# Written order around the norms, and the MLP up projection's products of high and low token parts 512 columns wide, with one pool of seven PSUM banks

## Chip, cores and metric

The program runs on one core of a Trainium2 chip. The metric is the device time of one launch in microseconds (us). Three runs of the kernel before gave 2601.47, 2604.80 and 2607.71 us; the median, 2604.8 us, is the time to compare with.

## What is computed

The reference is one inference step of a two-layer backbone in fp32 on 256 tokens: 128 context tokens (group g = 0) and 128 sample tokens (g = 1), width 2048. In each layer, cut to what matters here:

```
h   = x * (1 + scale1[g]) + shift1[g]          # from adaLN, six vectors per layer and group
mix = concat(attention(h @ w_in), hgrn2(h @ w_in))
y   = LayerNorm(alpha * x + gate1[g] * (mix @ w_o))
h2  = y * (1 + scale2[g]) + shift2[g]
f   = relu(h2 @ w_up) ** 2                     # 2048 -> 8192
x   = LayerNorm(alpha * y + gate2[g] * (f @ w_down))
```

The six adaLN vectors are `c @ w_mod + b_mod` for the two groups' conditioning vectors. The output is the last x and the new attention cache and scan states.

## The kernel before

**Products.** Every fp32 product is made of three fp32r products: an operand is split into a high part (rounded to fp32r) and a low part (the rest), and TensorE adds high·high, high·low and low·high into one PSUM tile. Weights come in items of 1 MB, two halves of 128x1024 each: DMA into `raw`, then `split` casts the high half on ScalarE (`wh`, L1328) and subtracts it on VectorE (`wl`, L1329). An item is 512 rows by 512 columns of a weight; a `Unit` is the items kg = 0 to 3 of one block of 512 columns. All items stand in one list, `seq`, and the loop at the end of the program walks through it; `main_ahead` puts the split of the next item ahead of the products of this one, as long as `raw` tiles (10) are free.

**Two kinds of unit.** In kind "T" (`mm_tile`, L445, L447, L448) the weights are loaded into the array and the 256 tokens move: per item 16 pairs of output block m and row block k, with three products of 256 columns each. The MLP's up projection and part of the in-projection are of this kind. In kind "N" (`n_tile`, L457 to L459) the tokens are loaded and 512 weight columns move: 24 products per item. w_o and the down projection are of this kind. Accumulators come from a pool of three PSUM banks (`accp`); one bank belongs to the adaLN products (`modp`), four to everything else (`sdp`).

**Order in a layer.** 13 units of in-projection with attention and scans as side tasks, w_o (in two passes over two items each), norm 1, MLP (four times four up units and four down units), norm 2. After the last layer norm 2 is `ln_last`. A w_o or down unit ends in `add_gated` or `d_down`: gate (L896), residual sum (L901), `bn_stats` (L891). There are three norms with `ln_mod`: norm 1 of layer 0, norm 2 of layer 0, norm 1 of layer 1, called first, second and third norm below. `ln_stat` aggregates the statistics (L909, and 1/sqrt at L621 to L627). Then for each quarter n of the width and each group: `ln_mod` normalises (L942), transposes on TensorE (L947), applies scale and shift (`scale_shift`: L929 on VectorE for group 0, L931 on ScalarE for group 1) and splits (`split_act`, L408 and L409). Quarter n is the token operand for the item kg = n of the next unit. All four quarters are written ahead of that unit.

**Other work.** adaLN products are items in the same list: `Mod` on TensorE (L203, `psm`, four products of 512 columns per 1 MB item) and `ModH` on VectorE (L266, `ma`). Rates spread them over the units; `flush` puts what a norm needs ahead of it, and `GAP` puts six of them after the first item behind a norm. `ln_out` is a side task that applies the norm's own gain and bias to the eight normalised tiles (16 VectorE operations of 128x512, L1013 and L1014), from rows that GpSimd's queue loads into two `G` tiles (L1007, L1008).

**Order on the engines.** SyncE and GpSimd run in the order of the program text. The orders of TensorE, VectorE and ScalarE are set by the framework's scheduler, apart from `ln_last`, which is written out.

## Time and profile before

| | before |
|---|---|
| median of three runs | 2604.8 us |
| the profiled execution | 2595.31 us |
| its span | 2593.4 us |
| TensorE busy (PE) | 2508.7 us, 97% |
| weight loads (PEld) | 2150.2 us, 83% |
| VectorE busy (DVE) | 1849.1 us, 71% |
| ScalarE busy (ACT) | 1227.5 us, 47% |
| mean granted TensorE clock | 0.989 |

The profile is that of one execution; its time is 9.5 us under the median of the runs. PE time is that of matmuls, PEld that of the weight loads that go beside them. A matmul's listed duration holds its way through the array, so neighbours overlap; what one costs in a row of them is the distance of starts.

### The profile page before, as it was taken

Reading aid. Unit: us, or ns where it says so; the run is one execution under the profiler, and the core shown is the slowest. Engines: PE = TensorE matmul, PEld = TensorE weight load, DVE = VectorE, ACT = ScalarE, POOL = GpSimd, SP = SyncE. Lnnn points to the kernel's source line nnn. Section 1 sums busy time; section 2 is a strip of 40 time slices with the busy share of each in tenths; the row PEclk is TensorE's granted clock in tenths of the full one; section 3 lists DMA queues with packets and bytes.
Section 4 is the critical chain, followed back from the end, with each engine's and each line's share of the span. In section 5 each row is a group of like instructions: output and inputs, shape, how many; then the busy total and the mean of one; then the engine's idle time right before and its main releaser. Section 6 shows DMA issues by size and latency. Waiting matters only on the chain.

```text
span 2593.4 us, 41149 instructions
## 1 busy us (share of the span) xinstructions
PE 2508.7 (97%) x16276; PEld 2150.2 (83%) x16276; DVE 1849.1 (71%) x2332; ACT 1227.5 (47%) x1703; POOL 105.0 (4%) x188
## 2 busy tenths in 40 slices
PE   7999899999999999999999999999899999999996
PEld 4787777768989879879877989788798998998985
DVE  3455778679887777887777788868865565666656
ACT  3434565435545444444435666744544454443542
POOL 2000000000000000000000010001000000000002
PEclk9999999999999999999999999999999999999998
DMA  9889778989987787887878576566576666666663
GB/s 357 271 285 321 268 246 284 325 277 359 315 295 274 267 292 269 285 276 263 288 234 292 193 243 197 193 221 223 187 235 218 212 215 217 217 200 227 204 206 115
DMA packets 192304, 652.77 MB, mean 252 GB/s; under 512 B 22720, under 2 KB 25344, under 8 KB 192112
## 3 DMA queue, kind: packets, MB, share of 16 engines
q1 hardware_dynamic: 177680, 614.56, 69.1%
q0 software_dynamic: 11488, 32.91, 4.3%
q8 instruction: 127, 2.08, 0.3%
q10 hardware_dynamic: 2944, 2.69, 0.3%
q14 instruction: 65, 0.53, 0.1%
HBM read 643.19 MB, written 6.88 MB: 251 GB/s over the span
## 4 chain that ended last, share of the span: by engine, by line
PE 61%; issue 28%; DMA 5%; DVE 4%; ACT 1%; POOL 0%; SPq 0%; POOLq 0%; DVEq 0%; ACTq 0%
PE acc L445 9%; PE acc L447 9%; PE acc L448 9%; PE acc L457 9%; PE acc L459 9%; PE acc L458 9%; DMA raw<-in_w_mod_dram 2%; PE psm L203 2%; DVE wl L1329 1%; PE psm L223 1%; DMA out_nsf_dram<-lf 1%; PE pI L757 1%; PE pX L780 1%; DMA raw<-in_w_in_dram 0%; PE pO L818 0%
## 5 line engine op out<-in xcount | busy, mean ns | idle before, releaser
L1328 ACT CAST wh<-raw 128x1024 fp32r<-128x1024 f32 x784 | 821.7, 1049 | 1065.3 <-PE acc L459 456.2
L1329 DVE TENSOR_TENSOR wl<-raw,wh 128x1024 fp32r<-128x1024 f32 x784 | 953.6, 1222 | 416.1 <-ACT wh L1328 397.1
L445 PE MATMUL acc<-hh,wh 128*128 128x256 f32 x3072 | 878.4, 286 | 3.0 <-DVE q L608 1.7
L448 PE MATMUL acc<-hh,wl 128*128 128x256 f32 x3072 | 871.3, 284 | 5.5 <-DVE wl L1329 5.5
L447 PE MATMUL acc<-hl,wh 128*128 128x256 f32 x3072 | 871.4, 284 | 0.0
L445 PEld LDWEIGHTS acc<-hh,wh 128*128 128x128 f32 x3072 | 589.9, 192 | 40.9 <-issue 31.2
L448 PEld LDWEIGHTS acc<-hh,wl 128*128 128x128 f32 x3072 | 589.9, 192 | 6.5 <-DVE wl L1329 6.5
L447 PEld LDWEIGHTS acc<-hl,wh 128*128 128x128 f32 x3072 | 590.2, 192 | 0.9 <-issue 0.2
L266 DVE SCALAR_TENSOR_TENSOR ma<-raw,stat,ma 128x1024 f32<-128x1024 f32 x300 | 378.6, 1281 | 95.0 <-DMA raw<-in_w_mod_dram 91.2
L458 PE MATMUL acc<-wl,fh 128*128 128x512 f32 x1024 | 399.4, 390 | 4.7 <-DVE wl L1329 4.7
L457 PE MATMUL acc<-wh,fh 128*128 128x512 f32 x1024 | 400.6, 391 | 1.8 <-DVE Z L1241 1.8
L459 PE MATMUL acc<-wh,fl 128*128 128x512 f32 x1024 | 398.9, 390 | 0.0
L457 PEld LDWEIGHTS acc<-wh,fh 128*128 128x128 f32 x1024 | 192.3, 188 | 51.0 <-issue 7.7
L458 PEld LDWEIGHTS acc<-wl,fh 128*128 128x128 f32 x1024 | 192.3, 188 | 45.4 <-DVE wl L1329 6.3
L459 PEld LDWEIGHTS acc<-wh,fl 128*128 128x128 f32 x1024 | 192.3, 188 | 40.0
L458 PE MATMUL acc<-wl,hh 128*128 128x512 f32 x320 | 129.4, 404 | 4.4 <-DVE wl L1329 4.4
L457 PE MATMUL acc<-wh,hh 128*128 128x512 f32 x320 | 131.3, 412 | 2.1 <-ACT hh L408 2.1
L459 PE MATMUL acc<-wh,hl 128*128 128x512 f32 x320 | 127.8, 402 | 0.0
L457 PE MATMUL acc<-wh,mxh 128*128 128x512 f32 x256 | 103.2, 404 | 0.0
L458 PE MATMUL acc<-wl,mxh 128*128 128x512 f32 x256 | 100.1, 392 | 0.0
L459 PE MATMUL acc<-wh,mxl 128*128 128x512 f32 x256 | 100.0, 392 | 0.0
L203 PE MATMUL psm<-raw,stat 128*2 128x512 f32 x640 | 95.0, 596 | 2.4 <-DMA raw<-in_w_mod_dram 2.4
(360 smaller groups left out, 1902.6 us busy)
## 6 DMA issues: line engine op xcount, KB each, us to landing
raw<-in_w_mod_dram SPq DMA_DIRECT2D x384, 512.0 KB
raw<-in_w_up_dram SPq DMA_DIRECT2D x256, 512.0 KB
raw<-in_w_down_dram SPq DMA_DIRECT2D x256, 512.0 KB
raw<-in_w_in_dram SPq DMA_DIRECT2D x208, 512.0 KB
raw<-in_w_o_dram SPq DMA_DIRECT2D x64, 512.0 KB
G<-gr POOLq DMA_DIRECT2D x48, 256.0 KB, 4.6
G<-in_lng_dram POOLq DMA_DIRECT2D x12, 256.0 KB, 5.9
G<-in_lnb_dram POOLq DMA_DIRECT2D x12, 256.0 KB, 5.7
```

The lines of the kernel that those rows point to most:

```text
L203: pe.matmul(self.ps[32 * j:32 * j + 2, :], lhsT=stat[:, k, :], rhs=raw[j // 2][:, 512 * (j % 2):512 * (j % 2) + 512], start=k == 0, stop=k ...
L223: pe.matmul(self.ps[32 * j:32 * j + 2, :], lhsT=stat[:, 4 * k + j, :], rhs=raw[j // 2][:, 512 * (j % 2):512 * (j % 2) + 512], start=k == 0 ...
L266: dve.scalar_tensor_tensor(self.acc[g], raw[h], c, self.acc[g], ALU.mult, ALU.add)
L445: pe.matmul(ps, lhsT=w0, rhs=hi[:, k], start=f and k == 0 and m % 2 == 0, stop=False, skip_group_check=True)
L447: pe.matmul(ps, lhsT=w0, rhs=lo[:, k], start=False, stop=False, skip_group_check=True)
L448: pe.matmul(ps, lhsT=w1, rhs=hi[:, k], start=False, stop=e and k == 3 and m % 2 == 1, skip_group_check=True)
L457: pe.matmul(ps, lhsT=hi[:, k, gs], rhs=wh[k], start=f and k == 0, stop=False)
L458: pe.matmul(ps, lhsT=hi[:, k, gs], rhs=wl[k], start=False, stop=False)
L459: pe.matmul(ps, lhsT=lo[:, k, gs], rhs=wh[k], start=False, stop=e and k == 3)
L757: pe.matmul(pI[:, 128 * m:128 * m + 128], lhsT=ke[:, 128 * m:128 * m + 128], rhs=qe[:, 128 * m:128 * m + 128], start=True, stop=True)
L1328: act.copy(wh, r)
L1329: dve.tensor_tensor(wl, r, wh.bitcast(F32), ALU.subtract)
```

## The change

1. The three-bank pool for accumulators is gone: accumulators come from `sdp`, which has seven banks.
2. A quarter of the token operand lies as two tiles of [128, 2 k, high or low, 256 tokens], so that the high and low tokens of one k are 512 neighbouring columns. A split of four blocks becomes two casts and two subtractions of half the size.
3. All up units but the first of each layer are of a new kind "W" (30 of 32). `w_tile` issues per pair of m and k one product of 512 columns (high weights by high and low tokens) and one of 256 (low weights by high tokens). Such a unit holds four banks; at its end ScalarE copies the low half of each (256 columns) and VectorE adds the two halves, before Relu, Square and split.
4. The last w_o unit and the last down unit of a layer are "tail" units: for group 1 their last products are issued in two halves of 256 columns, and `add_gated` follows in halves. Statistics of group 1 are always taken in halves.
5. The `flush` ahead of a norm stands before the tail unit, and no rate applies within it. From the last item of the tail unit to the last item of the following unit VectorE and ScalarE are put in written order (`ordered`). `ln_mod` is called once per quarter: quarters 0 and 1 ahead of the first item, 2 ahead of the second, 3 ahead of the third. For quarter 0 ScalarE normalises group 0 and writes the high parts from PSUM (L1002), VectorE makes scale and shift (L1007) and the low parts (L1012).

The core of the diff:

```diff
-    accp = ctx.enter_context(tc.tile_pool(name="accp", bufs=3, space=PS))
-    sdp = ctx.enter_context(tc.tile_pool(name="sdp", bufs=4, space=PS))
+    sdp = ctx.enter_context(tc.tile_pool(name="sdp", bufs=7, space=PS))
...
+    def w_tile(un, m, ks, hl, wh, wl, f, e):
+
+        if f and ks[0] == 0:
+            un.ps[m] = bank("acc")
+        ps = un.ps[m]
+        for k in ks:
+            x = hl[k // 2][:, k % 2]
+            w0, w1 = (w[k][:, 128 * m:128 * m + 128] for w in (wh, wl))
+            pe.matmul(ps, lhsT=w0, rhs=x.rearrange("p a t -> p (a t)"), start=f and k == 0, stop=False,
+                      skip_group_check=True)
+            pe.matmul(ps[:, 0:256], lhsT=w1, rhs=x[:, 0], start=False, stop=e and k == 3, skip_group_check=True)
...
+    def add_gated(key, n, g, ps, gt, first, last, tail):
+
+        for cols in halves(g) if tail else [slice(0, 512)]:
+            t = gt[:, cols]
+            dve.tensor_tensor(t, ps[:, cols], t, ALU.mult)
...
+    def ln_mod(key, AB, dst, n):
...
+        if first:
+            act.activation(y[0], y[0], AF.Identity, scale=mr[0][1], bias=nb)
+        for g in (1,) if first else (1, 0):
+            dve.tensor_scalar(y[g], y[g], mr[g][0], mr[g][1], ALU.subtract, ALU.mult)
...
+        else:
+            for c in range(4):
+                for g in (1, 0):
+                    act.activation(hl[c // 2][:, c % 2, 0, 128 * g:128 * g + 128], pt[g][:, 128 * c:128 * c + 128], AF.Identity,
+                                   scale=A[:, 4 * n + c, g:g + 1], bias=B[:, 4 * n + c, g:g + 1])
...
     def put_unit(un, rate, src=None, prate=0):
+        opening = closing = False
+        if norm:
+            key, coef, dst = norm[0][:3]
+            opening, closing = un.tail, not un.tail
         for kg in un.groups:
+            if opening and kg == un.groups[-1]:
+                AB = []
+                put_call(drain)
+                put_call(lambda: AB.append(ln_coef(*coef)))
+                put_call(lambda: ordered(True))
+                norm[0] += (AB,)
+            if closing:
+                AB = norm[0][3]
+                if kg == 0:
+                    put_call(lambda: ln_open(key))
+                    put_call(lambda: ln_mod(key, AB[0], dst, 0))
+                if kg < 3:
+                    put_call(lambda kg=kg: ln_mod(key, AB[0], dst, kg + 1))
+                else:
+                    norm.pop()
             seq.append(("main", Main(un, kg)))
+            if closing and kg == 3:
+                put_call(lambda: ordered(False))
...
-                    act.activation(r, un.ps[b], AF.Relu)
+                    if un.kind == "T":
+                        act.activation(r, un.ps[b], AF.Relu)
+                    else:
+                        low = u("e1")
+                        for j in range(2):
+                            ps, c = un.ps[2 * b + j], slice(256 * j, 256 * j + 256)
+                            act.copy(low[:, c], ps[:, 256:512])
+                            dve.tensor_tensor(r[:, c], ps[:, 0:256], low[:, c], ALU.add)
+                        act.activation(r, r, AF.Relu)
```

What this does to the engines' queues is seen at three places. In the changed kernel's numbering L988 is the normalisation on VectorE, L965 and L967 are scale and shift, L413 and L414 the split of tokens, L1086 and L1087 the operations of `ln_out`, L1435 and L1436 the split of weights, L994 the transpose.

First place: VectorE in the third norm, from the normalisation of group 1's first quarter to the second item's weights. Before (1793 and following), word for word:

```order
L942 TENSOR_SCALAR Y_17151<-Y_17151,s_17914,s_17918 128x512
L942 TENSOR_SCALAR Y_17273<-Y_17273,s_17914,s_17918 128x512
L942 TENSOR_SCALAR Y_17269<-Y_17269,s_17914,s_17918 128x512
L929 TENSOR_SCALAR ed_17948<-pt_17943,A_17909,B_17910 128x128 x4
L409 TENSOR_TENSOR hl_17928<-ed_17936,hh_17927 128x4x128
L942 TENSOR_SCALAR Y_17462<-Y_17462,s_17914,s_17918 128x512
L409 TENSOR_TENSOR hl_17928<-ed_17948,hh_17927 128x4x128
```

And now:

```order
L988 TENSOR_SCALAR Y_16319<-Y_16319,s_17269,s_17273 128x512
L1086 TENSOR_TENSOR Y_16319<-Y_16319,G_18093 128x512
L1087 TENSOR_TENSOR Y_16319<-Y_16319,G_18094 128x512
L1086 TENSOR_TENSOR Y_16315<-Y_16315,G_18093 128x512
L1087 TENSOR_TENSOR Y_16315<-Y_16315,G_18094 128x512
L1007 TENSOR_SCALAR ed_17289<-pt_17288,A_17205,B_17206 128x128
L1007 TENSOR_SCALAR ed_17295<-pt_17294,A_17205,B_17206 128x128
```

The first four operations of `ln_out` stand between the first normalisation and the first scale and shift. Before, the first of the sixteen stood behind all scale and shift operations and all token splits of the norm. In the first and third norm all sixteen now lie between the statistics and the fourth item's weights, four per quarter; in the second norm four do.

Second place: the same queue from the second item's weights into the third quarter of the third norm, now:

```order
L1436 TENSOR_TENSOR wl_17353<-raw_17043,wh_17352 128x1024
L1436 TENSOR_TENSOR wl_17357<-raw_17045,wh_17356 128x1024
L988 TENSOR_SCALAR Y_16580<-Y_16580,s_17269,s_17273 128x512
L988 TENSOR_SCALAR Y_16576<-Y_16576,s_17269,s_17273 128x512
L1086 TENSOR_TENSOR Y_16580<-Y_16580,G_18619 128x512
L1086 TENSOR_TENSOR Y_16576<-Y_16576,G_18619 128x512
L1087 TENSOR_TENSOR Y_16580<-Y_16580,G_18620 128x512
L1087 TENSOR_TENSOR Y_16576<-Y_16576,G_18620 128x512
L414 TENSOR_TENSOR ha_17414<-ed_17419,ha_17414 128x2x128
L414 TENSOR_TENSOR hb_17415<-ed_17419,hb_17415 128x2x128
L965 TENSOR_SCALAR ed_17425<-pt_17424,A_17205,B_17206 128x128 x4
L414 TENSOR_TENSOR ha_17414<-ed_17425,ha_17414 128x2x128
```

Behind the last row stands one more L414 and then the two operations of the third item's weights. So the weights of the second item stand behind all of quarter 1, those of the third behind all of quarter 2, those of the fourth behind all of quarter 3. In the first and second norm, where six adaLN items follow the first item, the weights of the second item too stand behind all of quarter 2. In all three norms TensorE has the sixteen transposes of quarters 0 and 1 ahead of the first product of the first item; those of quarter 2 stand behind that item, and in the first and second norm also behind most of the six adaLN items.

Third place: TensorE in the second item of the second up unit of layer 1, two and three pairs of m and k. Before:

```order
L445 MATMUL acc_18835<-hh_17955,wh_18823 128x256
L447 MATMUL acc_18835<-hl_17956,wh_18823 128x256
L448 MATMUL acc_18835<-hh_17955,wl_18824 128x256
L445 MATMUL acc_18848<-hh_17955,wh_18823 128x256
L447 MATMUL acc_18848<-hl_17956,wh_18823 128x256
L448 MATMUL acc_18848<-hh_17955,wl_18824 128x256
```

And now:

```order
L484 MATMUL acc_17698<-ha_17320,wh_17681 128x512
L486 MATMUL acc_17698<-ha_17320,wl_17682 128x256
L484 MATMUL acc_17703<-ha_17320,wh_17681 128x512
L486 MATMUL acc_17703<-ha_17320,wl_17682 128x256
L484 MATMUL acc_17703<-ha_17320,wh_17681 128x512
L486 MATMUL acc_17703<-ha_17320,wl_17682 128x256
```

Two products of 256 columns have become one of 512; the third is unchanged.

## Rows read from the trace of the kernel before

**Rows 1.** Page, part 1: busy us (share of the span) and instructions of each engine.

```profile
PE 2508.7 (97%) x16276; PEld 2150.2 (83%) x16276; DVE 1849.1 (71%) x2332; ACT 1227.5 (47%) x1703; POOL 105.0 (4%) x188
```

**Rows 2.** Page, part 5: costliest groups: line, engine, operation xcount | busy, mean ns | idle before.

```profile
L1329 DVE TENSOR_TENSOR wl<-raw,wh 128x1024 fp32r<-128x1024 f32 x784 | 953.6, 1222 | 416.1 <-ACT wh L1328 397.1
L445 PE MATMUL acc<-hh,wh 128*128 128x256 f32 x3072 | 878.4, 286 | 3.0 <-DVE q L608 1.7
...
L445 PEld LDWEIGHTS acc<-hh,wh 128*128 128x128 f32 x3072 | 589.9, 192 | 40.9 <-issue 31.2
```

**Rows 3.** Timeline of PE in an up unit: start, duration, line.

```profile
799.72 0.28 PE L445 MATMUL acc<-hh,wh 128*128 128x256 f32 x1
799.84 0.28 PE L447 MATMUL acc<-hl,wh 128*128 128x256 f32 x1
```

**Rows 4.** Timeline of PE around the first norm, from w_o's last products to the fourth up item.

```profile
590.07 0.39 PE L457 MATMUL acc<-wh,mxh 128*128 128x512 f32 x1
...
590.52 0.39 PE L459 MATMUL acc<-wh,mxl 128*128 128x512 f32 x1
...
602.46 0.48 PE L445 MATMUL acc<-hh,wh 128*128 128x256 f32 x2
...
621.84 0.28 PE L445 MATMUL acc<-hh,wh 128*128 128x256 f32 x1
```

**Rows 5.** The same around the second norm, to the second unit of layer 1.

```profile
1359.94 0.39 PE L459 MATMUL acc<-wh,fl 128*128 128x512 f32 x1
...
1398.62 0.28 PE L445 MATMUL acc<-hh,wh 128*128 128x256 f32 x1
```

**Rows 6.** The same around the third norm.

```profile
1836.41 0.39 PE L459 MATMUL acc<-wh,mxl 128*128 128x512 f32 x1
...
1848.06 0.51 PE L445 MATMUL acc<-hh,wh 128*128 128x256 f32 x2 [0.36 <-ACT hh L408]
...
1849.18 0.36 PE L447 MATMUL acc<-hl,wh 128*128 128x256 f32 x1
```

**Rows 7.** Busy by stretch: us, engines' busy us (instructions), granted clock, DMA share, GB/s.

```profile
591.00:603.00 12.00, 11.08 (x76) 4.17 (x69) 10.04 (x25) 5.69 (x16) 0.54 (x1) 1.00 1.02 408
603.00:640.00 37.00, 37.00 (x310) 35.19 (x308) 35.44 (x44) 24.07 (x33) 0.54 (x1) 1.00 0.98 359
640.00:980.00 340.00, 338.00 (x2109) 296.57 (x2105) 278.60 (x256) 156.52 (x174) 7.77 (x15) 1.00 0.84 289
...
1360.00:1372.00 12.00, 10.47 (x75) 3.91 (x74) 11.12 (x28) 4.84 (x13) 3.02 (x6) 1.00 0.96 348
1836.60:1849.20 12.60, 5.32 (x32) 4.71 (x31) 11.78 (x27) 5.95 (x14) 0.62 (x2) 0.73 0.56 199
```

**Rows 8.** Timeline of DVE in the third norm.

```profile
1841.05 0.26 DVE L909 BATCH_NORM_AGGREGATE s<-bs 128x2 f32<-128x24 f32 x1
...
1842.82 2.83 DVE L942 TENSOR_SCALAR Y<-Y,s,s 128x512 f32<-128x512 f32 x6
1845.56 1.37 DVE L929 TENSOR_SCALAR ed<-pt,A,B 128x128 f32<-128x128 f32 x4
```

**Rows 9.** Groups by shape, as in rows 2.

```profile
L266 DVE SCALAR_TENSOR_TENSOR ma<-raw,stat,ma 128x1024 f32<-128x1024 f32 x300 | 378.6, 1281 | 95.0 <-DMA raw<-in_w_mod_dram 91.2 <-ACT ma L264 3.6
...
L1014 DVE TENSOR_TENSOR Y<-Y,G 128x512 f32<-128x512 f32 x16 | 10.9, 689 | 1.0 <-DMA G<-in_lnb_dram 1.0
...
L863 DVE TENSOR_TENSOR Z<-Z,Z 128x256 f32<-128x256 f32 x8 | 3.1, 422 | 0.1
```

**Rows 10.** Timeline of POOL behind the first norm.

```profile
589.94 0.54 POOL L1007 DMA_DIRECT2D G<-in_lng_dram  x1 [8.81 <-DVE Y L901]
592.66 0.54 POOL L1008 DMA_DIRECT2D G<-in_lnb_dram  x1 [2.19 <-DVE Y L901]
```

**Rows 11.** Page, part 6: loads of those rows: xcount, KB, median us to landing.

```profile
G<-in_lnb_dram POOLq DMA_DIRECT2D x12, 256.0 KB, 5.7
```

More of the change, by code (lines that the diff above doesn't have):

```diff
@@ L48, with __init__ @@
 class Unit:
-    def __init__(self, kind, src, act, done, groups=range(4)):
+    def __init__(self, kind, src, act, done, groups=range(4), tail=False):
         self.kind = kind
+        self.tail = tail
         self.src = src
@@ L427, in mm_tile @@
                     between()
-                n_tile(un, g, range(4), hi, lo, wh, wl, f, e)
+                if g == 1 and un.tail:
+                    for h in range(2):
+                        n_tile(un, g, range(4), hl, wh, wl, f, e, slice(256 * h, 256 * h + 256))
+                else:
+                    n_tile(un, g, range(4), hl, wh, wl, f, e)
             return
@@ L449, in mm_tile, with n_tile @@
+                    pe.matmul(ps, lhsT=w1, rhs=x[:, 0], start=False, stop=e and k == 3 and m % 2 == 1,
                               skip_group_check=True)
[L451 removed]
+    def n_tile(un, g, ks, hl, wh, wl, f, e, cols=slice(0, 512)):
         if f and ks[0] == 0:
[L453 to L454 removed]
+            un.ps[g] = bank("acc")
+        ps = un.ps[g][:, cols]
         gs = slice(128 * g, 128 * g + 128)
+        skip = un.tail
@@ L886, in gate_chunk, with halves, stats @@
         return t
-    def stats(key, n, g):
-        if n == 0:
-            bst[key, g] = sp.tile([128, 24], F32, tag="bs", name=nm("bs"), bufs=4)
-        dve.bn_stats(bst[key, g][:, 6 * n:6 * n + 6], yt[key, n, g])
-    def add_gated(key, n, g, ps, gt, first, last):
-        t = gt
-        dve.tensor_tensor(t, ps, gt, ALU.mult)
-        y = yt[key, n, g]
-        if first:
-            dve.scalar_tensor_tensor(y, y, ALPHA, t, ALU.mult, ALU.add)
-        else:
-            dve.tensor_tensor(y, y, t, ALU.add)
-        if last:
-            stats(key, n, g)
+    def halves(g):
+        return [slice(0, 512)] if g == 0 else [slice(0, 256), slice(256, 512)]
+    def stats(key, n, g, h=0):
+        m = len(halves(g))
+        if n == 0 and h == 0:
+            bst[key, g] = sp.tile([128, 24 * m], F32, tag=f"bs{g}", name=nm("bs"), bufs=2)
+        c0 = 6 * (m * n + h)
+        dve.bn_stats(bst[key, g][:, c0:c0 + 6], yt[key, n, g][:, halves(g)[h]])
+    def add_gated(key, n, g, ps, gt, first, last, tail):
+        for cols in halves(g) if tail else [slice(0, 512)]:
+            t = gt[:, cols]
+            dve.tensor_tensor(t, ps[:, cols], t, ALU.mult)
+            y = yt[key, n, g][:, cols]
+            if first:
+                dve.scalar_tensor_tensor(y, y, ALPHA, t, ALU.mult, ALU.add)
+            else:
+                dve.tensor_tensor(y, y, t, ALU.add)
+            if last and tail:
+                stats(key, n, g, cols.start // 256)
+        if last and not tail:
+            for h in range(len(halves(g))):
+                stats(key, n, g, h)
     def ln_stat(key):
```

149 lines of the change are left out of this document (90 added, 59 removed).

## The prediction, written before the changed kernel ran

> **What bounds the kernel now.** I read the shares of busy time first: TensorE is busy for 97% of the span, VectorE for 71%, ScalarE for 47% [rows 1]. So time is won by making TensorE's work shorter, and lost wherever TensorE is made to stand; an idle microsecond of it is hardly ever given back. Next the groups by line, for what fills TensorE: the largest group has 3072 products of 256 columns, and it stands for three such lines, with a weight load of 192 ns for each [rows 2]. Listed durations (286 ns) overlap, so I take prices from distances of starts: 0.12 us for a product of 256 columns [rows 3], and 0.225 to 0.23 for one of 512 (590.07 to 590.52 is two) [rows 4]; I use 0.227. The weight load is longer than 0.12, yet the products follow each other at 0.12, so it is hidden.
>
> Then the busy time by stretch, for where TensorE does not run. In the MLP it does (338.0 of 340 us), with VectorE at 278.6 [rows 7]. In the first and second norm it hardly stops either (11.08 and 10.47 of 12 us), because adaLN products fill the hole; VectorE is the fuller engine, with 35.44 of 37 us in the unit behind the first norm. In the third norm, where none are left, TensorE works 5.32 of 12.6 us and its granted clock is 0.73 there, while VectorE works 11.78 [rows 7]. What decides around a norm is thus VectorE's queue.
>
> Last the timeline of the three norms, for the length of each stretch from the last product ahead of the norm (its start plus 0.23: 590.75, 1360.17, 1836.64) to the end of the unit behind it. First norm: the fourth item starts at 621.84 and has 48 products, 5.8 us, so 627.6; 36.9 us [rows 4]. Second: the next unit's first product is at 1398.62; 38.5 us [rows 5]. Third: two products from 1848.06, then 190 at 0.12 from 1849.18, so 1872.0; 35.3 us [rows 6]. Together 110.7 us.
>
> **Term 1, wider products.** 30 units of 4 items with 16 pairs of m and k are 1920 pairs of 256-column products that become one of 512. Each saves 2 x 0.12 - 0.227 = 0.013 us [rows 3, 4], or 25 us in all. Both distances fit a fixed 0.013 us per product beside the columns' own time, and 1920 products go. I take -25.
>
> The Trainium skill, "TensorE: Matmul & The Clock Gate", section "Wait — 56ns, not 53.3ns?", has a rule that speaks against so much: start to start is the column count over 2.4 GHz plus 2.5 ns. By it the two prices would be 109 and 216 ns and the term only -4.8 us, an estimate from that page. The trace disagrees: its starts lie 120 ns apart.
>
> **Term 2, the evacuation of the wide units.** Per unit four VectorE additions of 256 columns, for which the nearest row is 0.422 us [rows 9]: 1.7 us, 51 us over 30 units, with as many ScalarE copies. It lies in VectorE's idle time in the MLP (61 of 340 us idle, rows 7; a unit is 22 us, 15 of them in a stretch of some 700). The cover holds as long as a bank is free in time: a unit takes four of seven banks, so the next unit's fourth bank waits for the first of this one. That bank is complete a quarter of an item's walk, about 2 us, before the unit ends, and wanted 2 us after, so about 4 us stand for one copy and one addition. Bounds: 0, and 15 us if each of the 30 units waits half a microsecond; I take +2, near the lower one. The first-unit kind, the split of tokens in smaller pieces and the merged pool elsewhere I cost at nothing: they are hidden beside the same products, with 5 us either way for the in-projection's side tasks, which now draw banks from the same pool.
>
> **Term 3, tail units.** Three units (and the final one) issue 12 more products each at 0.013: +0.6. In return the last gate, sum and statistics run in halves; but both halves lie in one bank and the order has them all behind the unit's last product, so nothing runs beside TensorE. At the end of the kernel nothing else moves.
>
> **Term 4, the written stretch.** The fourth item of the unit behind a norm needs `wl`, and in VectorE's queue everything of the norm now stands ahead of that, the operations of `ln_out` too. In order, an operation of the queue can't pass another, so the sum of the queue is a floor. Prices in a run: a mean less 0.05 of overlap, or a timeline's group over its count. For the third norm: 6 halves x 0.37 [rows 9] = 2.2; from the aggregate to the first normalisation 1.77 [rows 8], with the second aggregate and the bias 2.0; 7 normalisations at 2.83 / 6 = 0.47, 3.3; 20 scale and shift operations at 1.37 / 4 = 0.34, 6.8 [rows 8]; 16 subtractions of 256 columns at 0.37, 5.9; 16 `ln_out` operations at 0.64, 10.2; 6 `wl` at 1.17 [rows 2], 7.0; 2 `ma` at 1.23 [rows 9], 2.5. Sum 39.9. The fourth item can start one `wl` earlier and takes 5.8: its end is at 44.5 us or later, where it was 35.3. First norm: no `ma` but the rest, 42.0 against 36.9. Second: four `ln_out` operations and eight `ma`, 39.6, with an item of 24 x 0.227 the end is 43.9 against 38.5. (The first stretch has one adaLN item fewer than before, the second one more, which cancels.) Floor of the three: 130.4 against 110.7, **+20**.
>
> The floor has no waits in it, and the written order has several. (a) The first four `ln_out` operations stand ahead of the first scale and shift. Their rows are loaded into the tiles of the last gate: the second load was issued when the last sum was done, 1.9 us behind the last product [rows 10], and lands 5.7 later at the median [rows 11]; with three operations behind it that is about 9.5 us. Scale and shift, subtractions, two normalisations and the transposes of quarter 1 (all ahead of the first product) bring the first item to some 15 us, where it was 11.7 in the first and 11.4 to 12.5 in the third norm [rows 4, 6]. (b) From there each quarter goes round: VectorE normalises, TensorE transposes, ScalarE scales and casts, VectorE subtracts, ScalarE casts the next item's weights behind that, VectorE subtracts them. VectorE's own part is 8.7 us per quarter (2 x 0.47, 4 x 0.64, 4 x 0.34, 4 x 0.37, 2 x 1.17), with one or two microseconds of waiting up to 10.5; TensorE's part is 5.8 for the item and one for transposes, so it stands for 2 to 4 us in each. The third norm: 13 + 3 x 10.5 + 2.5 - 1.2 + 5.8 = 51.6, loss 16. (c) In the first norm quarter 2's transposes stand behind the first item and most of six adaLN items (15 + 5.8 + 6), and the second item's weights behind all of that quarter: second item at about 36, then quarter 3 in the same way, end at about 56, loss 19. In the second norm most adaLN items run ahead of the first item: loss about 11. Together +46. Nearest to what the trace shows is a value between: VectorE in these stretches is 94 to 96% busy now [rows 7] in an order that a scheduler fitted to it; a fixed one with waits will be less, so I take nearer the upper end, **+39**. The moved `flush` costs nothing by itself (the same products, earlier), but in the first norm it no longer fills the hole; that is in the figure. `ln_out` leaving the MLP gives nothing back, since it was hidden there. Behind longer holes the clock may fall as in the third norm (0.73 [rows 7]); 0 to 8 us, I take +2.
>
> **Sum.** -25 + 2 + 0.6 + 39 + 2 = +19 on the profiled execution's 2595.3 us, so 2614 for one like it. That execution is 9.5 us under the median of the runs, so against the median I forecast 2604.8 + 19 = **2624 us**: slower.
>
> **Rivals.**
> *The order costs little (faster).* The mechanism: the tail's halves, ScalarE's direct writing of quarter 0 and the early transposes bring the first item forward, and later quarters hide behind products. For it: the third norm now leaves TensorE 7 us idle, and a gap shortened there is worth that. Against it: the sum of VectorE's queue, which holds without any wait. It decides if the three stretches lose under 20 us together; with a loss of 5 the time is 2604.8 - 25 + 5 = 2585. Chance 0.22.
> *At the floor.* VectorE never waits, and the loss is 20: 2600 to 2605. For it: VectorE's 35.44 of 37 us. Chance 0.15.
> *The wide units wait for banks or VectorE.* In layer 0 VectorE's 82% leave little room for 1.7 us more per unit at its end; with the upper bound of 15 the time is 2637. TensorE's waits for `wl` would show it. Chance 0.08.
> *The merge gives little.* If a product's fixed part is not 13 ns but a fifth of it, term 1 is -5 and the time 2644. Chance 0.05; the two distances of starts speak against it. This is the rule of the Trainium skill named above, and the row decides against it.
>
> **From cases to numbers.** The forecast's case, a loss of 30 to 55 around the norms, has 0.50. About 0.2% (5 us) is what a measurement can tell from no change: 2600 to 2610. The floor's case lies on its edge, so a third of it counts as faster and nearly all of the rest as no change. Faster 0.22 + 0.04 = 0.26, no change 0.12, slower 0.62. The range reaches from the better part of the first rival, 2585, to the bank case and the merge's failure at 2648; some 0.1 lies below and 0.06 above. The likeliest case alone is 2612 to 2642.
>
> **What would show it.** Right: products of 512 columns in up units 0.227 us apart, those of 256 0.12; the MLP between norms about 25 us shorter in all, with TensorE as full as now; the three stretches from the last product to the unit's end at 52, 56 and 50 us where they were 35.3, 36.9 and 38.5 (third, first, second); VectorE waiting for rows of G or for ScalarE in them, TensorE for `wl` ahead of the second to fourth items. Wrong: stretches under 44 us, which would say that the queue is not in the order that I read or that its operations are cheaper; up units that wait for banks; or a MLP no shorter than before.

## The result, and the profile after

The changed kernel took 2632.15 us (median of 4 runs, 2623.64 to 2634.04) where the kernel before took 2603.14 us on the same chip (4 runs, 2598.17 to 2607.71): a ratio of 1.0105, 95% interval 1.0076 to 1.0135. It is slower by 29 us; the forecast was slower by 19, with 2624 in a range of 2585 to 2648.

The shares of busy time in the page of the changed kernel, against [rows 1]:

```profile
PE 2504.7 (95%) x14404; PEld 2059.4 (78%) x14404; DVE 1898.8 (72%) x2528; ACT 1268.9 (48%) x1866; POOL 105.0 (4%) x188
```

There are 1872 matmuls fewer in the trace and TensorE's busy time is 4 us shorter, but the span is 36.3 us longer (2629.7 against 2593.4): TensorE stands 40 us more. (The medians are 29 us apart; the profiled execution before was 7.8 us faster than its median, that of the changed kernel stood at its own.) Where it stands, by the waits of TensorE over the whole span (engine, line, waited for: us in total, times, longest):

```profile
PE pt L994 <- DVE Y L988: 24.0, 4, 6.8
...
PE acc L458 <- ACT wh L1435: 10.8, 3, 5.5
...
PE pt L994 <- DVE Z L988: 6.5, 2, 4.5
...
PE acc L472 <- ACT wh L1435: 5.1, 2, 4.9
...
PE acc L484 <- DVE t L1327: 2.5, 2, 1.6
```

The first and third rows are transposes of the norms that wait for a normalisation, the second and fourth an item of the unit behind a norm that waits for its weights' high part. Together 46 us; before there were 7.3 of the former kind and none of the latter. The last row is all that wide units wait for VectorE's additions: 2.5 us.

The table splits both spans at the starts of products. A norm stretch reaches from the last product ahead of the norm to the last product of the first unit behind it; "MLP" is from there to the last down product of the layer; "rest" is all else (the start, the in-projections but their unit behind the second norm, w_o and the end).

| us | first stretch | second | third | sum of three | MLP, layer 0 | MLP, layer 1 | rest | span |
|---|---|---|---|---|---|---|---|---|
| before | 37.0 | 38.5 | 36.0 | 111.4 | 732.5 | 699.4 | 1050.1 | 2593.4 |
| changed | 57.2 | 54.9 | 51.2 | 163.4 | 717.2 | 690.0 | 1059.1 | 2629.7 |
| difference | +20.3 | +16.5 | +15.3 | +52.0 | -15.2 | -9.4 | +9.0 | +36.3 |

The busy time by stretch shows the same three (columns as in [rows 7]), before and then changed:

```profile
590.50:627.50 37.00, 36.08 (x282) 27.79 (x281) 33.76 (x56) 22.58 (x39) 0.54 (x1) 1.00 1.02 391
1359.90:1398.40 38.50, 34.84 (x178) 23.47 (x177) 34.97 (x61) 19.96 (x36) 3.02 (x6) 0.96 0.93 330
1836.40:1872.40 36.00, 28.72 (x226) 27.91 (x225) 31.48 (x59) 20.23 (x37) 2.44 (x5) 0.91 0.48 162
```

```profile
590.70:648.00 57.30, 39.05 (x275) 32.16 (x274) 41.00 (x84) 24.37 (x48) 7.72 (x15) 0.82 0.61 218
1365.20:1420.20 55.00, 38.62 (x186) 24.88 (x185) 40.83 (x78) 22.17 (x45) 3.06 (x6) 0.88 0.70 244
1867.70:1919.00 51.30, 32.90 (x227) 31.51 (x226) 42.34 (x84) 24.93 (x48) 7.59 (x15) 0.80 0.43 138
```

VectorE worked 87 to 91% of these stretches before and now works 72 to 83%: it waits too. The granted clock is 0.80 to 0.88 there, where it was 1.00, 0.96 and 0.91; with holes of 4 to 7 us in TensorE's work it falls to the lower of its two levels (1.2 GHz) in all three norms. The chain can be followed in VectorE's timeline of the third norm:

```profile
1872.49 0.54 DVE L988 TENSOR_SCALAR Y<-Y,s,s 128x512 f32<-128x512 f32 x1
1874.24 0.69 DVE L1086 TENSOR_TENSOR Y<-Y,G 128x512 f32<-128x512 f32 x1 [1.21 <-PE pt L994]
...
1877.33 2.67 DVE L1007 TENSOR_SCALAR ed<-pt,A,B 128x128 f32<-128x128 f32 x8 [0.34 <-ACT hb L1002]
...
1881.25 1.00 DVE L988 TENSOR_SCALAR Y<-Y,s,s 128x512 f32<-128x512 f32 x2
...
1888.40 2.36 DVE L1436 TENSOR_TENSOR wl<-raw,wh 128x1024 fp32r<-128x1024 f32 x2
1890.67 1.00 DVE L988 TENSOR_SCALAR Y<-Y,s,s 128x512 f32<-128x512 f32 x2
1893.22 1.29 DVE L1086 TENSOR_TENSOR Y<-Y,G 128x512 f32<-128x512 f32 x2 [1.54 <-PE pt L994]
...
1899.08 2.36 DVE L1436 TENSOR_TENSOR wl<-raw,wh 128x1024 fp32r<-128x1024 f32 x2 [0.52 <-ACT wh L1435]
1901.36 2.48 DVE L266 SCALAR_TENSOR_TENSOR ma<-raw,stat,ma 128x1024 f32<-128x1024 f32 x2
1903.75 1.00 DVE L988 TENSOR_SCALAR Y<-Y,s,s 128x512 f32<-128x512 f32 x2
...
1911.05 4.63 DVE L1436 TENSOR_TENSOR wl<-raw,wh 128x1024 fp32r<-128x1024 f32 x4 [0.52 <-ACT wh L1435]
```

The normalisation of quarter 1 (1881.25) starts when quarter 0's low parts are done, those of quarters 2 and 3 (1890.67, 1903.75) when the weights of the item before, or the `ma` behind them, are done. The weights of each quarter's own item follow 7.2, 8.4 and 7.3 us later. TensorE's timeline shows what that does to it:

```profile
1867.60 0.28 PE L474 MATMUL acc<-wh,mxb 128*128 128x256 f32 x1
1873.09 1.97 PE L994 MATMUL pt<-ident,Y 128*128 128x128 f32 x8 [5.21 <-DVE Y L988]
1881.85 1.97 PE L994 MATMUL pt<-ident,Y 128*128 128x128 f32 x8 [6.80 <-DVE Y L988]
1883.47 0.56 PE L458 MATMUL acc<-ha,wh 128*128 128x256 f32 x1
...
1899.11 0.39 PE L458 MATMUL acc<-ha,wh 128*128 128x256 f32 x1 [1.06 <-ACT wh L1435]
...
1911.07 0.39 PE L458 MATMUL acc<-ha,wh 128*128 128x256 f32 x1 [4.29 <-ACT wh L1435]
```

The wait of 6.80 us is for quarter 1's transposes, which the first item behind them does not need; it starts 15.9 us after the last product, where it was 11.65 before [rows 6].

### The profile page after: what moved, and what is told of

Its sections match the earlier page's. It is cut to its first block, busy times and chain, and to the rows that moved or that the text cites. A ratio compares the mean times of both kernels' runs of the same rounds, so it can differ in the third digit from the quotient of the medians.

```text
span 2629.7 us, 37793 instructions
## 1 busy us (share of the span) xinstructions
PE 2504.7 (95%) x14404; PEld 2059.4 (78%) x14404; DVE 1898.8 (72%) x2528; ACT 1268.9 (48%) x1866; POOL 105.0 (4%) x188
## 5 line engine op out<-in xcount | busy, mean ns | idle before, releaser
L1435 ACT CAST wh<-raw 128x1024 fp32r<-128x1024 f32 x784 | 819.7, 1049 | 975.5 <-PE acc L474 462.7
L1436 DVE TENSOR_TENSOR wl<-raw,wh 128x1024 fp32r<-128x1024 f32 x784 | 952.2, 1222 | 413.7 <-ACT wh L1435 399.1
L484 PE MATMUL acc<-ha,wh 128*128 128x512 f32 x960 | 345.5, 400 | 2.5 <-DVE t L1327 2.5
L484 PE MATMUL acc<-hb,wh 128*128 128x512 f32 x960 | 344.8, 399 | 0.0
L486 PE MATMUL acc<-ha,wl 128*128 128x256 f32 x960 | 269.8, 281 | 0.0
L486 PE MATMUL acc<-hb,wl 128*128 128x256 f32 x960 | 269.7, 281 | 0.0
L473 PE MATMUL acc<-wl,fb 128*128 128x512 f32 (+1 forms) x516 | 200.3, 388 | 1.1 <-DVE wl L1436 1.1
L472 PE MATMUL acc<-wh,fa 128*128 128x512 f32 (+1 forms) x516 | 201.1, 390 | 0.0
L472 PE MATMUL acc<-wh,fb 128*128 128x512 f32 (+1 forms) x516 | 200.5, 389 | 0.0
L473 PE MATMUL acc<-wl,fa 128*128 128x512 f32 (+1 forms) x516 | 200.2, 388 | 0.0
L474 PE MATMUL acc<-wh,fb 128*128 128x512 f32 (+1 forms) x516 | 200.0, 388 | 0.0
L474 PE MATMUL acc<-wh,fa 128*128 128x512 f32 (+1 forms) x516 | 200.0, 388 | 0.0
L458 PE MATMUL acc<-ha,wh 128*128 128x256 f32 x576 | 170.4, 296 | 10.8 <-ACT wh L1435 10.8
L461 PE MATMUL acc<-ha,wl 128*128 128x256 f32 x576 | 165.8, 289 | 2.4 <-DVE wl L1436 2.4
L460 PE MATMUL acc<-ha,wh 128*128 128x256 f32 x576 | 166.3, 289 | 0.0
L458 PE MATMUL acc<-hb,wh 128*128 128x256 f32 x576 | 165.8, 288 | 0.0
L460 PE MATMUL acc<-hb,wh 128*128 128x256 f32 x576 | 164.2, 285 | 0.0
```

Of the source, the lines that this page charges most:

```text
L458: pe.matmul(ps, lhsT=w0, rhs=x[:, 0], start=f and k == 0 and m % 2 == 0, stop=False, skip_group_check=True)
L460: pe.matmul(ps, lhsT=w0, rhs=x[:, 1], start=False, stop=False, skip_group_check=True)
L461: pe.matmul(ps, lhsT=w1, rhs=x[:, 0], start=False, stop=e and k == 3 and m % 2 == 1, skip_group_check=True)
L472: pe.matmul(ps, lhsT=hi, rhs=wh[k][:, cols], start=f and k == 0, stop=False, skip_group_check=skip)
L473: pe.matmul(ps, lhsT=hi, rhs=wl[k][:, cols], start=False, stop=False, skip_group_check=skip)
L474: pe.matmul(ps, lhsT=lo, rhs=wh[k][:, cols], start=False, stop=e and k == 3, skip_group_check=skip)
```

## The experiments

Two theories stood at first. One: the written order costs the norm stretches their 52 us, and the wide units do gain. The other: the wide units and the shared pool eat their own gain. Then: what of the written order costs, the sum of VectorE's queue or the hand-overs between engines?

The same table for all runs. Ratios below are to the kernel before, run beside each; e7, e8, e10 and e11 ran once each, the others 4 to 10 times. A row is one profiled execution, and a difference of some 8 us in "rest" is seen between executions whose code there is the same (e4 and e9), so only larger ones are read from that column.

| us | first stretch | second | third | sum of three | MLP, layer 0 | MLP, layer 1 | rest | span |
|---|---|---|---|---|---|---|---|---|
| e1 wide units, norms as before | 41.0 | 42.2 | 43.0 | 126.3 | 716.7 | 689.7 | 1061.5 | 2594.2 |
| e2 changed, narrow units | 57.2 | 53.0 | 51.3 | 161.5 | 730.9 | 696.4 | 1058.0 | 2646.8 |
| e3 changed, `ln_out` behind | 55.9 | 51.1 | 48.7 | 155.8 | 722.4 | 695.2 | 1065.9 | 2639.2 |
| e4 changed, order free | 36.9 | 39.0 | 37.2 | 113.1 | 717.5 | 690.0 | 1057.9 | 2578.5 |
| e5 changed, normalised first | 52.3 | 41.9 | 40.2 | 134.3 | 715.2 | 690.0 | 1059.5 | 2599.1 |
| e6 changed, adaLN ahead | 59.1 | 58.1 | 51.3 | 168.5 | 717.0 | 690.0 | 1061.0 | 2636.5 |
| e7 changed, products grouped | 58.1 | 54.1 | 51.2 | 163.4 | 716.9 | 685.2 | 1066.0 | 2631.5 |
| e8 e1 with narrow units | 41.4 | 40.2 | 44.5 | 126.2 | 736.9 | 696.4 | 1061.9 | 2621.4 |
| e9 e4 and e7 | 36.9 | 39.5 | 37.2 | 113.6 | 717.4 | 685.2 | 1066.0 | 2582.1 |
| e10 before, seven banks | 42.4 | 42.1 | 42.3 | 126.8 | 734.4 | 696.4 | 1066.6 | 2624.1 |
| e11 before, new token layout | 39.0 | 34.7 | 35.5 | 109.2 | 735.9 | 697.3 | 1051.1 | 2593.5 |

### e1: the wide units alone

```diff
-                put_call(drain)
-                put_call(lambda: AB.append(ln_coef(*coef)))
-                put_call(lambda: ordered(True))
...
+        put_call(drain)
+        put_call(lambda: ln_mod(k1, ln_coef(l, 4, 3, 2 * l), h2))
```

> The changed kernel with the norms, tail units and statistics of the kernel before: only the wide up units, the new layout of token tiles and the pool of seven banks are left. In the changed kernel's trace four wide units took 90.3 us where four narrow ones took 92.0, so a pair saves 6.7 ns. Theory A (the merge is worth 0.43 us per unit and the norms lose the rest): 30 units give -13 us, so about 2590 where the kernel before has 2603, with the three norm stretches at 37, 38 and 35 us as before. Rival B (banks and VectorE's additions eat the gain, and what the MLP gained in the changed kernel came from the operations of ln_out having left it): within 3 us of the kernel before. By the 2.5 ns per product of the Trainium skill's page "TensorE: Matmul & The Clock Gate" it would be -5; the rows of the trace decide.

Ratio 1.0019 (1.0005 to 1.0033): as slow as the kernel before, as rival B said, but not for its reason. The MLP did win, 15.8 and 9.7 us; the norm stretches (126.3 against 111.4) and the rest (+11.4) took it back, though the norms are written as before but for the token layout and the pool. That led to e8, e10 and e11.

### e2: the written order alone

```diff
-                put_unit(Unit("T" if sc == 0 and i == 0 else "W", lambda kg, nb=4 * sc + i: a["w_up"][l, nb, kg], lambda kg: h2[kg], d_up(i)),
+                put_unit(Unit("T", lambda kg, nb=4 * sc + i: a["w_up"][l, nb, kg], lambda kg: h2[kg], d_up(i)),
```

> The changed kernel with every up unit narrow (kind T); tails, written order and the pool of seven banks stay. Theory A: slower than the changed kernel by 30 x 0.43 = 13 us, about 2645, with norm stretches unchanged at 57, 55 and 51 us. Rival B (the MLP's gain is not the merge's): within 4 us of the changed kernel, 2632.

Ratio 1.0227 (1.0209 to 1.0246), 2654.8 us: theory A's direction, with more than its 13 us. By stage the MLP is 13.7 and 6.4 us longer than in the changed kernel. In layer 1 that is 15 units at 0.43 us; in layer 0, where VectorE is fuller, TensorE also stands longer (6.7 us against 3.7) and its clock falls to 1.2 GHz for 6.8 us. So the wide units are worth 20 us here, and the norm stretches hardly depend on them (161.5).

### e3: the operations of `ln_out` behind the written stretch

```diff
+            for _ in range(2):
+                dve.memset(u("G")[:, 0:1], 0.0)
             region[0].__exit__(None, None, None)
```

> The changed kernel, with two small writes to the G tiles at the end of the written stretch, so that the rows for ln_out are loaded behind it and its sixteen operations leave VectorE's queue between the statistics and the fourth item. Theory Q (VectorE's queue is the sum, as the prediction had it): the first and third norm lose 16 x 0.64 = 10 us of queue each, the second 2.6: 8 to 10 us shorter in each of the two, in all -18, about 2614. Rival C (hand-overs: in the trace these operations lie in time in which VectorE would wait for ScalarE anyway; L1007 waits for the last L1002 still): 2 to 3 us in each of the two, in all -5, about 2627.

Ratio 1.0168 (1.0152 to 1.0185): slower than the changed kernel. The stretches shrank by 1.3, 3.8 and 2.5 us, which is near rival C (in the second a wait for the rows of G went too, see term 4); theory Q, for which 8 to 10 us had to go in the first and third, falls. VectorE's waits between 1870 and 1925 us of this run say why:

```profile
DVE ha L414 <- ACT ha L413: 7.0, 3, 2.6
DVE wl L1438 <- ACT wh L1437: 4.3, 5, 1.4
DVE ed L1007 <- ACT hb L1002: 4.3, 1, 4.3
```

Without `ln_out` between them, VectorE's operations wait for ScalarE's. Neither theory had what came then: the sixteen operations now stand in the MLP, and it is 5.2 us longer in both layers. The operations alone don't cost that: in e4, where the scheduler put 14 and 6 of the sixteen in the MLP of layers 0 and 1, it is as short as in the changed kernel. In the three up units behind the third stretch TensorE waits 3.1 us for the evacuation of a wide unit, where the changed kernel has no wait of TensorE in those units at all.

### e4: the order left to the scheduler

```diff
     def ordered(on):
 
-        if on:
-            region[0] = tc.manual_schedule(engines={mybir.EngineType.DVE, mybir.EngineType.Activation})
-            region[0].__enter__()
-        else:
-            region[0].__exit__(None, None, None)
+        pass
```

> The changed kernel without the written stretch: the calls stand where they stood, one quarter ahead of its item, but the scheduler sets VectorE's and ScalarE's order. Theory W (the written order is what costs): the norm stretches come back to within 5 us of 37, 38 and 35, so some 40 us less, about 2592. Rival P (the place of the calls costs: quarter 2's transposes behind the first item and the adaLN items, no adaLN products left for the hole): less than 12 us of the 52 come back, 2620 or more.

Ratio 0.9951 (0.9934 to 0.9967), 2586.4 us: theory W. The stretches come back to 36.9, 39.0 and 37.2 us, 50.3 of the 52.0. Everything else of the change is still there. In VectorE's timeline of the third norm the scheduler has all seven normalisations in a row, and TensorE sixteen transposes at once:

```profile
1836.76 3.28 DVE L988 TENSOR_SCALAR Y<-Y,s,s 128x512 f32<-128x512 f32 x7
```

```profile
1837.35 3.68 PE L994 MATMUL pt<-ident,Y 128*128 128x128 f32 x16 [6.65 <-DVE Y L988]
```

Both kernels are beaten by this one: faster by 0.3 to 0.7% than before.

### e5: written order, but all normalisations first

```diff
-        for g in (1,) if first else (1, 0):
-            dve.tensor_scalar(y[g], y[g], mr[g][0], mr[g][1], ALU.subtract, ALU.mult)
+        if first:
+            for m in range(4):
+                for g in (1,) if m == 0 else (1, 0):
+                    z = yt[key, m, g]
+                    dve.tensor_scalar(z, z, mr[g][0], mr[g][1], ALU.subtract, ALU.mult)
```

> The changed kernel, written order kept, but with the normalisations of all four quarters ahead of the first item; the transposes of quarters 2 and 3 then also come ahead of it. The queue of VectorE has the same operations as before this edit, only seven of them stand earlier. Theory H (hand-overs: each quarter's normalisation stands behind the weights of the item before, its transposes behind that item, and the item after it waits for one whole round): the third stretch goes from 51 to about 44 us, the first from 57 to about 47 (the second item no longer waits for quarter 2's transposes behind the adaLN items), the second from 55 to about 49; in all -23, about 2609. Rival Q (the sum of VectorE's queue sets the end): the queue is as long as it was, so the three stretches together change by less than 8 us, 2625 or more.

Ratio 1.0030 (1.0016 to 1.0044), 2607.5 us. The three stretches fell by 29.1 us in all, where theory H had 23 and theory Q less than 8. The same operations are done; six of them stand earlier, and with them the transposes of quarters 2 and 3. The first stretch gained least (57.2 to 52.3 instead of 47), and for a reason that neither theory had: the second item's weights come late. In the waits of SyncE's queue (590 to 640 us) and of ScalarE (595 to 648 us):

```profile
SPq L1420 <- PE psm L203: 24.3, 5, 22.9
```

```profile
ACT wh L1438 <- DMA raw<-in_w_up_dram: 11.1, 4, 10.0
```

The adaLN items that stand behind the first item on TensorE hold `raw` tiles, SyncE stands 22.9 us for one, and ScalarE then stands 10.0 us for the weights that were asked for so late. In the changed kernel SyncE stands even longer at this place (26.1 us), but there ScalarE casts those weights right behind quarter 2's split, so the order binds first. So more than half of the loss (29.1 of 52.0 us) is shown to be hand-overs; of the 21.2 us that remain against e4, 15.4 lie in the first stretch, where late weights are part of it.

### e6: the adaLN items ahead of the transposes

```diff
-    GAP = 6
+    GAP = 0
...
                 if kg == 0:
+                    put_mods(6)
                     put_call(lambda: ln_open(key))
```

> The changed kernel with the six adaLN items that follow the first item of a norm's unit put ahead of the norm's transposes instead, into the hole in which TensorE stands 5.5 and 7.2 us. Theory H: TensorE's adaLN work (about 6 us) then lies in the hole and quarter 2's transposes stand behind the first item alone: first stretch 57 to about 48, the second a few us less, the third as it was; about 2621. Rival (the transposes now stand behind the adaLN products, whose weights come late): the first stretch stays within 3 us, 2630 or more.

Ratio 1.0152 (1.0127 to 1.0176); the first stretch grew by 1.9 us and the second by 3.2: the rival. The adaLN products do run in the first hole, but the transposes stand behind them in TensorE's queue, so the round starts later by what they take, and the second hole is as long as it was:

```profile
PE acc L458 <- ACT wh L1436: 6.8, 2, 4.9
PE pt L994 <- DVE Y L988: 6.8, 1, 6.8
PE psm L203 <- issue: 3.3, 1, 3.3
```

(TensorE's waits between 585 and 660 us.) Filling a hole helps only where the chain that makes the hole doesn't stand behind the filling.

### e7: products grouped by width

```diff
         for k in ks:
             x = hl[k // 2][:, k % 2]
-            w0, w1 = (w[k][:, 128 * m:128 * m + 128] for w in (wh, wl))
-            pe.matmul(ps, lhsT=w0, rhs=x.rearrange("p a t -> p (a t)"), start=f and k == 0, stop=False,
-                      skip_group_check=True)
-            pe.matmul(ps[:, 0:256], lhsT=w1, rhs=x[:, 0], start=False, stop=e and k == 3, skip_group_check=True)
+            pe.matmul(ps, lhsT=wh[k][:, 128 * m:128 * m + 128], rhs=x.rearrange("p a t -> p (a t)"),
+                      start=f and k == 0, stop=False, skip_group_check=True)
+        for k in ks:
+            x = hl[k // 2][:, k % 2]
+            pe.matmul(ps[:, 0:256], lhsT=wl[k][:, 128 * m:128 * m + 128], rhs=x[:, 0], start=False,
+                      stop=e and k == 3, skip_group_check=True)
```

> The changed kernel with another order of products in a wide unit: for the two k of a half first both products of 512 columns, then both of 256. Four wide units take 90.33 us now, 0.353 us per pair of m and k; 0.227 + 0.120 would give 88.9. If the missing 6 ns come from the alternation of a wide and a narrow product, four units take 89.6 or less; if each wide product followed by another weight load costs them, 90.3 stays.

Four wide units took 89.05 us instead of 90.33: the alternation it is. TensorE's timelines of the changed kernel and of e7, in an up unit of layer 1:

```profile
2099.64 0.40 PE L484 MATMUL acc<-hb,wh 128*128 128x512 f32 x1
2099.88 0.28 PE L486 MATMUL acc<-hb,wl 128*128 128x256 f32 x1
2099.99 0.40 PE L484 MATMUL acc<-hb,wh 128*128 128x512 f32 x1
2100.24 0.28 PE L486 MATMUL acc<-hb,wl 128*128 128x256 f32 x1
```

```profile
2099.74 0.63 PE L483 MATMUL acc<-hb,wh 128*128 128x512 f32 x2
2100.21 0.39 PE L487 MATMUL acc<-hb,wl 128*128 128x256 f32 x2
2100.44 0.63 PE L483 MATMUL acc<-hb,wh 128*128 128x512 f32 x2
```

Two pairs take 0.70 us grouped; alternating, the starts lie 0.23 to 0.25 and 0.11 or 0.12 apart, and the mean over four units (256 pairs) is 90.33 / 256 = 0.353 against 89.05 / 256 = 0.348. The narrow three products take 92.03 / 256 = 0.359. The one run took 2633.4 us, no different from the changed kernel's runs.

### e8, e10 and e11: pool and layout apart

e8 is e1 with every up unit narrow. The edits of e10 (against the kernel before) and e11 (against e8):

```diff
-    accp = ctx.enter_context(tc.tile_pool(name="accp", bufs=3, space=PS))
-    sdp = ctx.enter_context(tc.tile_pool(name="sdp", bufs=4, space=PS))
+    sdp = ctx.enter_context(tc.tile_pool(name="sdp", bufs=7, space=PS))
...
-            un.ps[g] = accp.tile([128, 512], F32, tag="acc", name=nm("acc"))
+            un.ps[g] = bank("acc")
```

```diff
+    accp = ctx.enter_context(tc.tile_pool(name="accp", bufs=3, space=PS))
-    sdp = ctx.enter_context(tc.tile_pool(name="sdp", bufs=7, space=PS))
+    sdp = ctx.enter_context(tc.tile_pool(name="sdp", bufs=4, space=PS))
...
-            un.ps[g] = bank("acc")
+            un.ps[g] = accp.tile([128, 512], F32, tag="acc", name=nm("acc"))
```

> As e1, but with narrow up units: against the kernel before only the token layout and the pool of seven banks are new. In e1 the three norm stretches took 41.0, 42.2 and 43.0 us and the two w_o stages 3 and 5 us more than before, which ate the 25 us that the MLP won. If layout and pool do that, it is seen here too: stretches of 41 to 43, w_o at 136 and 105, MLP as in e2 (731 and 696), a time of some 2615 to 2620. If it comes from the order that the scheduler happened to set for e1, the stretches lie near 37, 38 and 36.

> The kernel before with one pool of seven banks in place of three and four; nothing else. In e8, which has the new layout of token tiles too, the norm stretches took 41.4, 40.2 and 44.6 us (37.0, 38.5 and 36.0 before) and the time rose by some 20 us. If the pool does that, the stretches sum to 120 or more here; if the layout does, they stay at 111 and the time at 2600.

> e8 with the two pools of the kernel before: only the layout of the token tiles is new, with casts and subtractions of half the size and twice the number. If the layout costs the norm stretches, they sum to 120 or more here (126.2 in e8) and the time is some 2615; if the pool does, 111 and 2600.

e8 took 2623.3 us, e10 2625.8, e11 2595.4 (one run each, beside a kernel before of 2600.0, 2598.3 and 2598.3). So the token layout with its halved operations costs nothing that one run shows, and the one pool alone costs some 27 us in its one run, where the kernel before had 2592 to 2606. In the profiled execution that is 15 more in the norm stretches (126.8 against 111.4) and 16 in the rest, with one back in the MLP.

The norm stretches agree in all three runs with the one pool and the norms written as before: 126.3, 126.2 and 126.8 us in e1, e8 and e10. What TensorE does there is the same in all nine of their stretches: all 32 transposes stand ahead of the first product of the next unit, which starts 17.3 to 19.7 us after the last product ahead of the norm. Before, 24 stood ahead and it started after 11.7 to 11.9 us; in e11, with the two pools back, 20 and 9.4 to 11.3 us. TensorE in the third norm, before and in e10 (last products at 1836.41 and 1863.82), and the VectorE row that e10's last four transposes wait for:

```profile
1843.51 4.18 PE L947 MATMUL pt<-ident,Y 128*128 128x128 f32 x24 [6.71 <-DVE Y L942]
```

```profile
1870.78 5.27 PE L946 MATMUL pt<-ident,Y 128*128 128x128 f32 x28 [6.58 <-DVE Y L941]
1881.29 1.09 PE L946 MATMUL pt<-ident,Y 128*128 128x128 f32 x4 [5.23 <-DVE Y L941]
1882.03 0.56 PE L444 MATMUL acc<-hh,wh 128*128 128x256 f32 x1
```

```profile
1880.61 0.54 DVE L941 TENSOR_SCALAR Y<-Y,s,s 128x512 f32<-128x512 f32 x1
```

VectorE is no later than before up to the normalisations: its second aggregate comes 4.6 us after the last product in both. But the first product now stands behind a normalisation that VectorE does only after scale and shift of earlier quarters, and TensorE waits 5.23 us for it. The first product is 6.3, 6.8 and 6.6 us later than before in e10's three norms, as much as the stretches lost or more (5.4, 3.6 and 6.3). That the pool costs is shown, and where; why the scheduler puts the first product behind all transposes when it draws from the one pool is open. The 16 in the rest are spread over both in-projections and both w_o, in one execution.

### e9: e4 and e7 together

> e4 and e7 together: the scheduler's order around the norms, and in wide units both products of 512 columns ahead of both of 256. e7 took 1.28 us off four wide units and 4.8 us off the MLP of layer 1 behind its first unit; if that adds to e4, which stood at 0.9951 of the kernel before, some 9 us more go: a ratio of 0.9915, about 2578 where the kernel before has 2600. If in e4 the up units wait for something else in layer 0 (weights, banks), layer 0 keeps its 717 us and only 5 go: 0.993.

Ratio 0.9936 (0.9921 to 0.9951), 2582.5 us, the lowest of the study; the expected 0.9915 lies just outside. Layer 1's MLP gave its 4.8 us, layer 0's stayed at 717.4, as the second case said. The rest was 8 us longer than in e4's profiled execution, with the same code there; between e4 and e9 the intervals overlap.

## Why the prediction was right, point by point

**The direction and the size** were right, 19 us forecast and 29 measured, and for the reason given: TensorE's gain in the MLP is smaller than what it loses in three norm stretches. e4 shows the cause by taking it away: 50 us of the 52 are the written order's. That the forecast came so near is in part luck. In the profiled executions the MLP gave -24.6, the stretches +52.0 and the rest +9.0: the first met its term by two mistakes, the second stood 11 us above its terms (39, and 2 for the clock), and the third, forecast at nothing, is no larger than what two executions of the same code can differ by.

**Term 1 (-25)** came out by two mistakes that cancel. The price of a pair was wrong: 6.7 ns saved and not 13 ([rows 3, 4] are distances in runs of equal products, and the change makes an alternation), 1920 x 0.0067 = 13 us. But the MLP won 24.6 us, because TensorE also waited less for weights. Its waits for `wl` in the MLP, before (layer 0, two rows, and layer 1) and changed (layer 0; in layer 1 there is none):

```profile
PE acc L458 <- DVE wl L1329: 4.7, 4, 3.6
PE acc L448 <- DVE wl L1329: 2.8, 3, 1.3
```

```profile
PE acc L448 <- DVE wl L1329: 2.7, 2, 1.5
```

```profile
PE acc L473 <- DVE wl L1436: 1.1, 1, 1.1
```

All waits of TensorE there went from 10.2 to 3.7 us in layer 0 and from 2.7 to none in layer 1. With 6.4 us of price in each layer and eight adaLN products fewer in layer 0 (some 1.8 us) that makes 14.7 of 15.2 and 9.1 of 9.4. The sentence that `ln_out` leaving the MLP gives nothing back fits e4 and not e3, where it cost 5.2 us in each layer: it depends on where the operations fall. The rule of the Trainium skill ("TensorE: Matmul & The Clock Gate", "Wait — 56ns, not 53.3ns?"), 2.5 ns a product, is not what the runs show: 6.7 ns a pair alternating, 11.6 ns grouped (92.03 - 89.05 over 256).

**Term 2 (+2)**: the evacuation is hidden, 2.5 us of waits for VectorE's additions. That the merged pool costs nothing beside ±5 us was the step that failed: e10 lost some 27 us by it alone, 15 of them in the norms. In the changed kernel and in e4, where `ln_mod` is called once per quarter, 16 transposes stand ahead of the first product and that part does not show. In the rest the changed kernel lost 9 us, where e8 and e10, with the pool, lost 12 and 16 and e11, without it, 1; these are single executions, so a part of the pool in the 9 is likely but not shown.

**Term 3 (+0.6)**: nothing runs beside TensorE in the tail's halves, as was said: the first half's gate starts at 1867.91, behind the last product of the second half (1867.60). In e4, where the order is free, the first item behind the norm starts 6.9, 7.4 and 10.3 us after the last product, where it was 11.9, 11.9 and 11.7. Its transposes start 1.5, 1.0 and 0.2 us earlier than before, and 16 of them stand ahead of the first product instead of 24; what the tails and ScalarE's part in quarter 0 add was not tried apart.

**Term 4 (+39)**: the stretches were put at 56, 50 and 52 us and measured 57.2, 54.9 and 51.2, a loss of 52.0 in all. The rounds in (b) and the transposes behind the adaLN items in (c) are what the traces show. Two steps were wrong. The floor by the sum of VectorE's queue is not what sets the end: e3 took the `ln_out` operations out of the queue and gained 1 to 4 us a stretch, e5 put six normalisations earlier and gained 29. And (a), the wait for rows of G, was laid in the wrong norm. In the first and third it did not happen: the loads landed after 3.8 and 3.6 us at the median, and the third norm's first `ln_out` operation waited for a transpose, 1.21 us. The first item came at 15.9 us all the same, because quarter 1's transposes stood ahead of it. In the second norm it did happen, for the rows of the second load, ahead of quarter 0's scale and shift:

```profile
1376.82 1.29 DVE L1087 TENSOR_TENSOR Z<-Z,G 128x512 f32<-128x512 f32 x2 [3.67 <-DMA G<-in_lnb_dram]
```

The first item came at 19.0 us there, and this is the norm that was mis-sized most: a loss of 16.5 us where 11 was forecast (20.3 for 19 and 15.3 for 16 in the others). The +39 was chosen between a floor of 20 and a sum by parts of 46; the sum by parts was the better reading, and still 6 short. The +2 for the clock was not measured apart: TensorE's busy time in the three stretches rose from 99.6 to 110.6 us for nearly the same products (686 and 688), so the lower clock can have taken some 11 of the 52 us, part of which other waits would have taken anyway.

**The rivals.** "The order costs little" named 2585 us; that is what the kernel takes when the order is not written (2586.4). The bank waits did not come, and the merge gave more than a fifth of its fixed part. The upper end of the likeliest case, 2642, is not what its terms add up to (2639 with a loss of 55); nothing hangs on it.

## What to carry to other kernels

A written order has to be read as rounds: count how often it hands work from engine to engine and back before the waiting engine may go on, and put what can be done at once for all pieces (here seven normalisations and their transposes) ahead of the first round. Work that fills an engine's wait costs little there and may cost more where it is moved to. A larger shared pool is not free where a scheduler sets the order: measure it alone, for it can eat a real gain elsewhere. And look at the load queue before calling a wait a matter of order: items that are put behind others keep the tiles that the next weights need.

## What the runs showed of the hardware that was not expected

A product of 512 columns followed by one of 256, each with a weight load of its own, takes 0.353 us a pair over four units; the same products in groups of two equal ones take 0.348. Next to that, runs of 256 columns have 0.120 us a product and runs of 512 have 0.227. What in the alternation costs the 5 ns is open.

The loads of G took 3.6 to 3.8 us at the median in the changed kernel, where the lnb loads took 5.7 in the kernel before [rows 11], though the one that the second norm waited for took some 9 (issued at 1367.85, its reader started at 1376.82); in the third norm DMA moved 138 GB/s then. Whether the lighter traffic is the cause was not tried.
